# VectorE in place of GpSimd for two groups of additions in the first product of a gMLP decoder kernel

## The chip, the cores and the metric

The kernel runs on one core of one Trainium2 chip. The metric is the device time of one execution in microseconds (us), and the time of a kernel is the median of several runs. In the rows PE is TensorE's matmul, PEld its weight load, DVE is VectorE, ACT is ScalarE, POOL is GpSimd and SP is SyncE, whose queue (SPq) issues loads.

## What is computed

A decoder trunk of two layers on x (1 x 2048 tokens x 1024 features). The first layer is the one that matters here:

```python
def rms_norm(x, g):
    y = x * rsqrt(mean(x * x, axis=-1, keepdims=True) + EPS) * g
    return y

def gmlp_mixer(h, w_in, ln_g, ln_b, ws, bs, w_out):      # h = rms_norm(x, a_norm_g)
    z = h @ w_in                                         # (2048 x 1024) @ (1024 x 6144)
    u, v, g = jnp.split(z, 3, axis=-1)                   # 2048 columns each
    v = layer_norm(v, ln_g, ln_b)
    v = v.reshape(b, nc, CHUNK, A_GROUPS, A_GROUP_DIM)   # chunks of 128 tokens, 16 groups of 128
    sv = jnp.einsum('gts,bcsgd->bctgd', tril(ws), v) + bs.T[:, :, None]
    y = u * sv.reshape(b, s, A_WIDTH) * silu(g)
    return y @ w_out

h = x + gmlp_mixer(rms_norm(x, a_norm_g), ...)
```

After it come one product for keys and values, a sliding-window attention layer with its own in and out products, and a last norm. The change lies wholly in the first tenth of the run: the product that makes v for the first 1024 tokens, and what is prepared beside it.

## The kernel before

**Layout.** Activations lie with features on the 128 partitions and 512 tokens in the free direction. The 2048 tokens are four blocks of 512; two blocks make a superblock, and the gMLP layer runs superblock by superblock. Every operand of a large product is held as two float32r parts, hi and lo, and each product is three matmuls: hi by hi (L122), hi by lo (L123), lo by hi (L124). Both parts of a weight tile `wa` are made from the loaded float32 tile `w_raw`: ScalarE casts hi (L118) and VectorE subtracts to get lo (L119). There are four buffers for `wa`, so a split runs at most four weights ahead of the matmuls that use it, and L123 cannot run before its weight's L119.

**The first v product** (`vphase_first`, L591 to L608) takes x unnormalized, as hi and lo parts `xh`, `xl` times the gain (made at L750 and L751), and the token scale 1/rms is put on afterwards when ScalarE copies the product out of PSUM (L605). It runs four column groups by two token blocks by eight feature tiles k: 64 weights of 128 x 512, with twelve matmuls each. After each group of eight weights ScalarE copies four banks out and VectorE takes their statistics (`bn_stats`, L607). The product runs from 5.5 to 233 us of the span.

**Work put beside it.** The calls `after(n, ...)` place work at half-steps of the product (one half-step per weight). The scheduler that builds the program then orders each engine's instructions by its own estimate; the order below is the one that it chose. Beside the first v product stand:

- the norm of the first and second token block. `first_stat` (L766 to L774) squares each of eight tiles on ScalarE and adds the squares; `rnorm` (L266 on) splits the sum (hi by ScalarE, lo by GpSimd at L119), sums over partitions on TensorE (L270, L271), and makes the reciprocal root per token, `r4` (L255 to L260), and as a 128 x 512 tile, `r0` (L277 to L289). For the first block the squares are added on VectorE (`sumsq_step`, L248), for the second on GpSimd (L770).
- `x_steps(0, k)` for k = 0 to 3 (L424 to L463): four normalized quarters of x are made in a tile `xq`, and `combos` (L365 to L383) writes three of them to HBM and makes sums and differences of them on GpSimd (L373, L375, L379, L381), each written by a DMA that GpSimd's queue issues (L367). There are two `xq` buffers, so the third and fourth k must wait for the last combination (L381) and the DMAs of the first and second. Each quarter is made in two steps: an addition of its hi and lo part (L451), and a product with r0 (L452, VectorE).
- `sum_job(i)`, four jobs (L465 to L488): GpSimd makes sums and differences of weight tiles `qa`, eight additions each (L479), written by four DMAs (L472).
- `load_consts` (L385 to L406): tables for the token mixing (a matmul L398, VectorE L401, DMAs L403).

`in_turn` (L757 to L763) makes the GpSimd additions that pass through it follow one another in the order in which the code names them: L479, L451 and L770.

Of the kernel before, what the change touches and what calls it, by code (L numbers as in the profile page):

```python
# [12 lines left out]
F32 = mybir.dt.float32  # L13
F32R = mybir.dt.float32r
I32 = mybir.dt.int32
AF = mybir.ActivationFunctionType
ALU = mybir.AluOpType
# [45 lines left out]
def trunk(ctx: ExitStack, tc: tile.TileContext, xT, wv, wug, wao, wkv, wqg, wbo, wsT, bs, gains, lngb,  # L63
          bq, bkv, sinks, rot, masks, out):
    nc = tc.nc
    V, A, G, PE = nc.vector, nc.scalar, nc.gpsimd, nc.tensor
# [21 lines left out]
    def load(dst, src):  # L88
        nc.sync.dma_start(dst, src)

    def slot(dt=F32):
        return gen[0].tile([P, TB], dt, name="s", tag="s")
# [69 lines left out]
    for b in range(NB):  # L162
        for p in PIECES:
            kind, i, j = p[0], int(p[1]), int(p[2])
# [78 lines left out]
    def sumsq_step(acc, src, eng=G):  # L243
        sq = slot()
        A.activation(sq, src, AF.Square)
        if acc is None:
            return sq
        eng.tensor_tensor(acc, acc, sq, ALU.add)  # L248
        return acc
# [83 lines left out]
    with ExitStack() as actx:  # L333
# [31 lines left out]
        def combos(q11, q12, q21, q22, key, k):  # L365

            put = lambda n, t: G.dma_start(setD[key][n][:, k], t)  # L367
            put("11", q11)
            put("12", q21)
            put("s4", q22)  # L370
            yield
            t1, t2 = slot(), slot()
            G.tensor_tensor(t1, q12, q11, ALU.subtract)  # L373
            put("s1", t1)
            G.tensor_tensor(t2, q22, t1, ALU.subtract)  # L375
            put("s2", t2)
            yield
            t3, t4 = slot(), slot()
            G.tensor_tensor(t3, q22, q12, ALU.subtract)  # L379
            put("s3", t3)  # L380
            G.tensor_tensor(t4, q21, t2, ALU.subtract)  # L381
            put("22", t4)
            yield  # L383
# [40 lines left out]
        def x_steps(sb, k, tag):  # L424

            qs, its = [], []

            def begin():
                if sb == 0:
                    t = xcg.tile([P, 2048], F32, name="xq", tag=tag)  # L430
                    qs.extend(t[:, i * TB:(i + 1) * TB] for i in range(4))
                else:
                    qs.extend(slot() for _ in range(4))
                if sb:
                    for i, z in enumerate(qs):
                        load(z, xT[2 + i // 2, k + 4 * (i % 2)])
                    rs.extend(slot() for _ in range(2))
                    for h in range(2):
                        load(rs[h], rxD[2 + h])
                else:  # L440
                    rs.extend(r0[h] for h in range(2))

            rs = []

            def norm(i):
                h, n = i // 2, k + 4 * (i % 2)
                if sb:
                    V.scalar_tensor_tensor(qs[i], qs[i], a_g[:, n:n + 1], rs[h], ALU.mult, ALU.mult)
                else:
                    hi, lo = fx[h, n]  # L450
                    in_turn(lambda: G.tensor_tensor(qs[i], hi.bitcast(F32), lo.bitcast(F32), ALU.add))  # L451
                    V.tensor_tensor(qs[i], qs[i], rs[h], ALU.mult)  # L452

            def norms(h):
                norm(2 * h)
                norm(2 * h + 1)

            def step():
                if not its:
                    its.append(combos(qs[0], qs[2], qs[1], qs[3], ("X", sb), k))  # L460
                next(its[0])

            return [begin, lambda: None, lambda: None, lambda: norms(0), lambda: norms(1), step, step, step]  # L463
# [290 lines left out]
        box = [None, None]  # L754
        gl = [None]

        def in_turn(fn):  # L757

            if gl[0] is None:
                gl[0] = fn().ins  # L760
                return
            with tc.issue_after(gl[0]):
                gl[0] = fn().ins  # L763


        def first_stat(h, k, t, wait):  # L766
            if h and box[1]:
                sq = slot()
                A.activation(sq, t, AF.Square)
                in_turn(lambda: G.tensor_tensor(box[1], box[1], sq, ALU.add))  # L770
            else:
                box[h] = sumsq_step(box[h], t, V)
            if k == KD - 1:
                rnorm(box[h], lambda r: r0.update({h: r}), wait, 4, lambda z: r4.update({h: z}))  # L774

# [7 lines left out]
        for k in range(KD):  # L783
            after(ST0 + k // 2, lambda k=k: first_stat(0, k, xs[k], 1))
        ys = []
        for k in range(KD):
            after(1 + k // 2, lambda k=k: ys.append(first_x(1, k)))
            after(3 + k // 2, lambda k=k: first_split(1, k, ys[k]))
            after(6 + k // 2, lambda k=k: first_stat(1, k, ys[k], 2))
# [350 lines left out]
    for b in range(NB):  # L1140
# [39 lines left out]
        for p in PIECES:  # L1180
            kind, i, j = p[0], int(p[1]), int(p[2])
# [79 lines left out]
```

## Time and profile before

| | us |
|---|---|
| median of 3 runs | 2227.95 |
| the runs | 2225.21, 2227.95, 2232.17 |
| the profiled execution, its time | 2234.51 |
| the profiled execution, its span | 2232.8 |
| TensorE busy in the span | 2141.1 |
| VectorE busy | 1669.6 |
| GpSimd busy | 1092.5 |

The profiled execution is one run of its own, 6.6 us above the median of the others. TensorE is busy in all but 92 us of the span, so a stretch is read by how far TensorE falls short of the stretch's length there, and by what ended each of its idle times. In the first v product TensorE falls short in four places, near 45, 60 to 120, 132 and 155 to 170 us; after 170 us it runs without a gap until the product's end.

### The profile page before, as it was taken

The page shows a single profiled execution, that of the slowest core. Times are in us where ns is not written, and L with a number is a line of the kernel's source. Part 1 is how long each engine was busy: PE and PEld are TensorE (multiplying, and loading weights), DVE is VectorE, ACT ScalarE, POOL GpSimd, SP SyncE. Part 2 cuts the span into 40 slices and gives each one's busy share as a digit, 9 for nine tenths or more (in the row PEclk, how much of TensorE's full clock was granted, in tenths as well). Part 3 has the DMA queues.
Part 4 walks back from the last instruction along what each step waited for, and adds up shares of the span by engine and source line. Part 5 has one row for each costly group of instructions (what it writes and reads, how often), then busy time and mean ns, then how long its engine had stood idle before and what let it go on. Part 6 is the DMA issues. An engine that isn't in the chain of part 4 may idle for free.

```text
span 2232.8 us, 33563 instructions
## 1 busy us (share of the span) xinstructions
PE 2141.1 (96%) x11196; PEld 1813.6 (81%) x11196; DVE 1669.6 (75%) x2670; ACT 1088.6 (49%) x2431; POOL 1092.5 (49%) x1201
## 2 busy tenths in 40 slices
PE   7879999999899989999999899999999999999997
PEld 6658888888688767788888788898899889889986
DVE  7946787788986865756656977578867967986785
ACT  6224654445444534444444533246635734663573
POOL 4892355767444555644544545334514622551460
PEclk9989999999999999999999999999999999999999
DMA  8987555667786789634444786633363355337322
GB/s 283 342 298 238 180 185 188 208 196 244 256 303 226 273 312 314 222 113 135 149 133 130 263 309 214 214 123 114 123 245 115 115 187 180 114 124 243 116 95 95
DMA packets 208941, 441.96 MB, mean 198 GB/s; under 512 B 22656, under 2 KB 61824, under 8 KB 199552
## 3 DMA queue, kind: packets, MB, share of 16 engines
q1 hardware_dynamic: 163488, 255.76, 35.6%
q0 software_dynamic: 40672, 175.66, 21.5%
q10 hardware_dynamic: 4608, 8.39, 1.0%
q8 instruction: 89, 1.46, 0.3%
q14 instruction: 84, 0.69, 0.1%
HBM read 322.81 MB, written 116.92 MB: 197 GB/s over the span
## 4 chain that ended last, share of the span: by engine, by line
PE 72%; DVE 10%; DMA 7%; issue 5%; POOL 4%; ACT 2%; SPq 1%; POOLq 0%; DVEq 0%; ACTq 0%
PE ps L130 13%; PE ps L129 13%; PE ps L128 13%; PE ps L122 8%; PE ps L123 8%; PE ps L124 8%; PE ps L635 2%; PE ps L1024 2%; DVE wa L119 1%; PE ps L971 1%; PE ps L1002 1%; PE ps L972 1%; PE ps L943 1%; DMA s<-Y 1%; POOL qa L479 1%
## 5 line engine op out<-in xcount | busy, mean ns | idle before, releaser
L119 DVE TENSOR_TENSOR wa<-w_raw,wa 128x512 fp32r<-128x512 f32 x456 | 478.7, 1059 | 148.0 <-ACT wa L118 147.0
L130 PE MATMUL ps<-xh,wa 128*128 128x512 f32 x1344 | 529.4, 394 | 14.7 <-DVE wa L119 14.7
L128 PE MATMUL ps<-xh,wa 128*128 128x512 f32 x1344 | 531.2, 395 | 0.6 <-DVE s L656 0.3
L129 PE MATMUL ps<-xl,wa 128*128 128x512 f32 x1344 | 528.2, 393 | 0.0
L118 ACT CAST wa<-w_raw 128x512 fp32r<-128x512 f32 x456 | 280.6, 619 | 433.0 <-PE ps L130 314.9
L130 PEld LDWEIGHTS ps<-xh,wa 128*128 128x128 f32 x1344 | 253.3, 188 | 74.8 <-DVE wa L119 18.4
L128 PEld LDWEIGHTS ps<-xh,wa 128*128 128x128 f32 x1344 | 253.6, 189 | 56.6 <-DVE s L656 0.8
L129 PEld LDWEIGHTS ps<-xl,wa 128*128 128x128 f32 x1344 | 253.6, 189 | 55.7
L1010 POOL TENSOR_SCALAR_AFFINE_SELECT s<-s 128x512 fp32r<-128x512 f32 x256 | 185.0, 750 | 101.5 <-ACT s L1004 70.2
L223 POOL TENSOR_TENSOR w_raw<-w_raw 128x512 f32<-128x512 f32 x48 | 78.6, 1639 | 224.5 <-DMA w_raw<-in_wug 121.7
L122 PE MATMUL ps<-w,hn 128*128 128x256 f32 x640 | 184.5, 288 | 0.0
L123 PE MATMUL ps<-w,hn 128*128 128x256 f32 x640 | 182.6, 285 | 0.0
L124 PE MATMUL ps<-w,hn 128*128 128x256 f32 x640 | 182.5, 285 | 0.0
L119 DVE TENSOR_TENSOR xl<-s,xh 128x512 fp32r<-128x512 f32 x168 | 137.7, 856 | 13.7 <-ACT xh L118 13.6
L190 POOL DMA_DIRECT2D w<-wb x72 | 40.5, 563 | 208.8 <-PE ps L124 177.7
L631 ACT ACTIVATE vp<-vp,nb,rs 128x128 f32<-128x128 f32 x256 | 106.6, 485 | 46.0 <-DMA vp<-v 39.1
L123 PE MATMUL ps<-wa,xh 128*128 128x512 f32 x256 | 107.1, 418 | 21.2 <-DVE wa L119 20.9
L996 POOL TENSOR_TENSOR s<-s,rd 128x512 f32<-128x512 f32 x64 | 69.5, 1088 | 114.8 <-ACT s L1004 46.6
L123 PEld LDWEIGHTS ps<-w,hn 128*128 128x128 f32 x640 | 124.4, 194 | 0.5
L122 PEld LDWEIGHTS ps<-w,hn 128*128 128x128 f32 x640 | 124.2, 194 | 0.5
L124 PEld LDWEIGHTS ps<-w,hn 128*128 128x128 f32 x640 | 124.2, 194 | 0.0
L225 POOL TENSOR_TENSOR w_raw<-w_raw 128x512 f32<-128x512 f32 x48 | 65.1, 1362 | 104.7 <-DVE wa L119 102.4
(192 smaller groups left out, 5007.6 us busy)
## 6 DMA issues: line engine op xcount, KB each, us to landing
w<-wb POOLq DMA_DIRECT2D x72, 1024.0 KB, 5.5
w_raw<-in_wug SPq DMA_DIRECT2D x160, 256.0 KB, 3.2
w_raw<-in_wv SPq DMA_DIRECT2D x88, 256.0 KB, 5.4
s<-in_xT SPq DMA_DIRECT2D x80, 256.0 KB, 4.7
w_raw<-in_wao SPq DMA_DIRECT2D x80, 256.0 KB, 4.2
wb<-s POOLq DMA_DIRECT2D x72, 256.0 KB, 5.1
vp<-v SPq DMA_DIRECT2D x32, 512.0 KB, 4.4
Y_s<-s POOLq DMA_DIRECT2D x64, 256.0 KB, 3.9
```

The lines of the kernel that those rows point to most:

```text
L118: A.copy(hi, src)
L119: (lo_eng or V).tensor_tensor(lo, src, hi.bitcast(F32), ALU.subtract)
L122: PE.matmul(ps, ah, bh, start=first, stop=False)
L123: PE.matmul(ps, ah, bl, start=False, stop=False)
L124: PE.matmul(ps, al, bh, start=False, stop=last)
L128: PE.matmul(ps, ah, bh, start=first, stop=False, skip_group_check=True)
L129: PE.matmul(ps, ah, bl, start=False, stop=False, skip_group_check=True)
L130: PE.matmul(ps, al, bh, start=False, stop=True, skip_group_check=True)
L223: G.tensor_tensor(u["22"], u["21"], u["22"], ALU.add)
L631: A.activation(v[:, c, :], v[:, c, :], AF.Identity, bias=nb[:, c:c + 1], scale=rs[:, c:c + 1])
L996: G.tensor_tensor(p4, p4, rd[:, :, None].broadcast_to([P, 4, P]), ALU.mult)
L1010: G.affine_select(out=y.rearrange("p (h q) -> p h q", h=4), in_=x.rearrange("p (h q) -> p h q", h=4), pattern=[[0, 4], [sign, P]], base=ba ...
```

## The change

Two groups of additions move from GpSimd to VectorE. In `x_steps` the sixteen additions L451 leave GpSimd's fixed turn. In `first_stat` the second block's seven square additions (L770 with the squares of L769) go through `sumsq_step` as the first block's do, and so to VectorE's L248 (squares at L245).

```diff
             def norm(i):
                 h, n = i // 2, k + 4 * (i % 2)
...
                     hi, lo = fx[h, n]
-                    in_turn(lambda: G.tensor_tensor(qs[i], hi.bitcast(F32), lo.bitcast(F32), ALU.add))
+                    V.tensor_tensor(qs[i], hi.bitcast(F32), lo.bitcast(F32), ALU.add)
                     V.tensor_tensor(qs[i], qs[i], rs[h], ALU.mult)
...
         def first_stat(h, k, t, wait):
-            if h and box[1]:
-                sq = slot()
-                A.activation(sq, t, AF.Square)
-                in_turn(lambda: G.tensor_tensor(box[1], box[1], sq, ALU.add))
-            else:
-                box[h] = sumsq_step(box[h], t, V)
+            box[h] = sumsq_step(box[h], t, V)
             if k == KD - 1:
                 rnorm(box[h], lambda r: r0.update({h: r}), wait, 4, lambda z: r4.update({h: z}))
```

Every engine's order of instructions changes in the first v product alone; behind it the orders are the same, line for line. Three places follow, each of the kernel before and then of the changed one. Counted from the product's first, the split that stands behind all these additions in the first place is the 12th.

VectorE where the second block's norm is made, some 31 to 50 us into the span. L282 is the end of the first block's norm, L255 the first step of the second block's that reads TensorE's sum. Before:

```order
L282 TENSOR_TENSOR s<-ident,r4h 128x512
L282 TENSOR_TENSOR s<-ident,r4l 128x512
L119 TENSOR_TENSOR wa<-w_raw,wa 128x512 x2
L607 BN_STATS bst<-s 128x6 x4
L119 TENSOR_TENSOR wa<-w_raw,wa 128x512 x3
L255 TENSOR_TENSOR s<-ps,ident 128x512
```

Changed, from behind the same two L282, two L119, the first two L248 and one L451, which alternate:

```order
L248 TENSOR_TENSOR s<-s 128x512
L607 BN_STATS bst<-s 128x6
L248 TENSOR_TENSOR s<-s 128x512
L607 BN_STATS bst<-s 128x6
L248 TENSOR_TENSOR s<-s 128x512
L607 BN_STATS bst<-s 128x6 x2
L451 TENSOR_TENSOR xq<-xh,xl 128x512 x3
L248 TENSOR_TENSOR s<-s 128x512
L451 TENSOR_TENSOR xq<-xh,xl 128x512
L248 TENSOR_TENSOR s<-s 128x512
L119 TENSOR_TENSOR wa<-w_raw,wa 128x512 x4
L255 TENSOR_TENSOR s<-ps,ident 128x512
```

Between the second L282 and the third of the weight splits L119 there stood two L119 and four L607; now there stand, with those ahead of the rows, two L119, four L607, seven L248 and five L451.

GpSimd in the same stretch; `su` are the sums in HBM, and the second L119 is the lo part of the second block's sum of squares. Before:

```order
L119 TENSOR_TENSOR s<-s 128x512
L260 TENSOR_TENSOR r_474<-m_471,neghalf 128x4
L770 TENSOR_TENSOR s<-s 128x512 x7
L479 TENSOR_TENSOR qa<-qa 128x512 x3
L119 TENSOR_TENSOR s<-s 128x512
L472 DMA su_0_153<-qa 128x1024
```

Changed:

```order
L260 TENSOR_TENSOR r_474<-m_471,neghalf 128x4
L479 TENSOR_TENSOR qa<-qa 128x512 x2
L472 DMA su_0_153<-qa 128x1024
L479 TENSOR_TENSOR qa<-qa 128x512 x3
L472 DMA su_2_155<-qa 128x1024
L479 TENSOR_TENSOR qa<-qa 128x512 x2
L472 DMA su_1_154<-qa 128x1024
L479 TENSOR_TENSOR qa<-qa 128x512
L119 TENSOR_TENSOR s<-s 128x512
L472 DMA su_3_156<-qa 128x1024
```

The first job's eight additions and three of its DMA issues now stand ahead of that L119, in the place of seven L770 and three L479.

VectorE from the 28th weight split of the product to the 35th, some 105 to 140 us into the span; L401 belongs to `load_consts`. Before, with the third k of `x_steps`:

```order
L119 TENSOR_TENSOR wa<-w_raw,wa 128x512 x4
L401 SCALAR_TENSOR_TENSOR s<-ps,lngb_sb,s 128x128 x4
L119 TENSOR_TENSOR wa<-w_raw,wa 128x512 x2
L452 TENSOR_TENSOR xq<-xq,s 128x512
L119 TENSOR_TENSOR wa<-w_raw,wa 128x512
L452 TENSOR_TENSOR xq<-xq,s 128x512 x3
L119 TENSOR_TENSOR wa<-w_raw,wa 128x512
L401 SCALAR_TENSOR_TENSOR s<-ps,lngb_sb,s 128x128 x4
```

Changed, with the fourth k:

```order
L119 TENSOR_TENSOR wa<-w_raw,wa 128x512 x4
L401 SCALAR_TENSOR_TENSOR s<-ps,lngb_sb,s 128x128 x4
L451 TENSOR_TENSOR xq<-xh,xl 128x512 x2
L452 TENSOR_TENSOR xq<-xq,s 128x512
L119 TENSOR_TENSOR wa<-w_raw,wa 128x512
L452 TENSOR_TENSOR xq<-xq,s 128x512
L451 TENSOR_TENSOR xq<-xh,xl 128x512 x2
L452 TENSOR_TENSOR xq<-xq,s 128x512
L119 TENSOR_TENSOR wa<-w_raw,wa 128x512
L452 TENSOR_TENSOR xq<-xq,s 128x512
L119 TENSOR_TENSOR wa<-w_raw,wa 128x512 x2
L401 SCALAR_TENSOR_TENSOR s<-ps,lngb_sb,s 128x128 x4
```

In this stretch stood the third k, and the fourth stood about the 41st split; now the fourth k stands here, beginning ahead of the 32nd split, the third about the 24th and 25th, and behind the rows no L451 or L452 is left. The additions of the third and fourth k, which now stand in VectorE's order, wait there for the buffer: for L381 and the DMAs of the first and the second k.

## Rows read from the trace of the kernel before

**Rows 1.** The page's head: the span, and busy time of each engine (share of the span, instructions).

```profile
span 2232.8 us, 33563 instructions
...
PE 2141.1 (96%) x11196; PEld 1813.6 (81%) x11196; DVE 1669.6 (75%) x2670; ACT 1088.6 (49%) x2431; POOL 1092.5 (49%) x1201
```

**Rows 2.** Stretches of the span: its start and end, its length, busy time of PE, PEld, DVE, ACT and POOL with their instructions, TensorE's granted clock (1.00 is 2.4 GHz), the mean share of the DMA engines, and GB/s.

```profile
60.00:80.00 20.00, 18.31 (x75) 13.54 (x74) 20.00 (x15) 6.63 (x11) 16.59 (x19) 1.00 1.01 357
80.00:100.00 20.00, 16.66 (x68) 12.27 (x66) 18.00 (x10) 4.70 (x8) 19.05 (x21) 1.00 0.97 339
100.00:120.00 20.00, 17.02 (x57) 12.58 (x58) 17.11 (x23) 3.90 (x7) 14.89 (x17) 0.83 0.97 332
120.00:140.00 20.00, 14.94 (x52) 11.31 (x52) 9.85 (x13) 5.01 (x8) 19.58 (x20) 0.83 0.90 307
140.00:160.00 20.00, 15.44 (x66) 11.92 (x64) 4.39 (x7) 6.25 (x10) 19.66 (x20) 0.98 0.95 347
160.00:180.00 20.00, 16.57 (x60) 13.29 (x61) 17.18 (x16) 2.48 (x4) 15.06 (x16) 0.77 0.62 208
180.00:200.00 20.00, 20.00 (x89) 16.41 (x88) 10.85 (x17) 10.31 (x18) 0.00 (x0) 1.00 0.71 233
31.00:170.00 139.00, 112.88 (x422) 85.44 (x421) 101.05 (x94) 37.96 (x64) 125.85 (x123) 0.89 0.87 299
```

**Rows 3.** Waits from 40 to 180 us: the engine, tile and line that waited, what it waited for, us in total, times, the longest.

```profile
DVE xq L452 <- POOL xq L451: 28.7, 3, 14.4
...
PE ps L123 <- DVE wa L119: 20.9, 8, 7.8
...
PE ps L271 <- POOL s L119: 3.7, 1, 3.7
```

**Rows 4.** The timeline of TensorE in a few short stretches: start in the span, duration, engine, line, operation, tiles, shape, and in brackets the idle time before it and what ended that.

```profile
43.60 0.50 PE L270 MATMUL ps<-s,inv_r 128*128 128x512 f32 x1 [1.34 <-ACT s L118]
...
48.30 0.80 PE L271 MATMUL ps<-s,inv_r 128*128 128x512 f32 x1 [3.73 <-POOL s L119]
...
122.08 0.39 PE L123 MATMUL ps<-wa,xh 128*128 128x512 f32 x1
...
132.84 0.80 PE L123 MATMUL ps<-wa,xh 128*128 128x512 f32 x1 [5.06 <-DVE wa L119]
...
163.43 0.79 PE L123 MATMUL ps<-wa,xh 128*128 128x512 f32 x1 [7.83 <-DVE wa L119]
164.02 0.63 PE L124 MATMUL ps<-wa,xl 128*128 128x512 f32 x1
164.45 0.63 PE L122 MATMUL ps<-wa,xh 128*128 128x512 f32 x1
...
169.14 0.46 PE L124 MATMUL ps<-wa,xl 128*128 128x512 f32 x1
169.44 0.39 PE L122 MATMUL ps<-wa,xh 128*128 128x512 f32 x1
169.68 0.39 PE L123 MATMUL ps<-wa,xh 128*128 128x512 f32 x1
```

**Rows 5.** Groups of instructions from 0 to 180 us: line, engine, operation, tiles, shapes, count, then busy us and mean ns of one, then the idle time just before them and what ended it.

```profile
L119 DVE TENSOR_TENSOR wa<-w_raw,wa 128x512 fp32r<-128x512 f32 x48 | 68.2, 1448 | 5.8 <-ACT wa L118 5.8
L479 POOL TENSOR_TENSOR qa<-qa 128x512 f32<-128x512 f32 x32 | 43.6, 1388 | 1.8 <-DMA qa<-in_wv 1.7
...
L451 POOL TENSOR_TENSOR xq<-xh,xl 128x512 f32<-128x512 f32 x16 | 22.9, 1452 | 0.1
L607 DVE BATCH_NORM_STATS2 bst<-s 128x6 f32<-128x512 f32 x20 | 12.6, 676 | 0.0
L770 POOL TENSOR_TENSOR s<-s 128x512 f32<-128x512 f32 x7 | 11.2, 1595 | 1.3 <-ACT s L769 0.8
L472 POOL DMA_DIRECT2D su<-qa x16 | 9.3, 583 | 0.6 <-POOL qa L479 0.6
...
L248 DVE TENSOR_TENSOR s<-s 128x512 f32<-128x512 f32 x7 | 4.8, 683 | 0.0
```

**Rows 6.** The timeline of GpSimd and then of VectorE about the second block's norm, as in rows 4 (xN: so many of a kind in a row, with the time of all).

```profile
31.26 11.64 POOL L770 TENSOR_TENSOR s<-s 128x512 f32<-128x512 f32 x7 [0.84 <-ACT s L769]
...
46.99 1.25 POOL L119 TENSOR_TENSOR s<-s 128x512 fp32r<-128x512 f32 x1
```

```profile
31.81 1.79 DVE L282 TENSOR_TENSOR s<-ident,r4l 128x512 fp32r<-128x512 f32 x1
33.52 3.47 DVE L119 TENSOR_TENSOR wa<-w_raw,wa 128x512 fp32r<-128x512 f32 x2
36.91 2.46 DVE L607 BATCH_NORM_STATS2 bst<-s 128x6 f32<-128x512 f32 x4
39.30 2.47 DVE L119 TENSOR_TENSOR wa<-w_raw,wa 128x512 fp32r<-128x512 f32 x2
```

**Rows 7.** The timeline of VectorE, then of GpSimd, at the third and fourth k and in the dense stretch ahead of them, as in rows 4.

```profile
71.71 12.72 DVE L119 TENSOR_TENSOR wa<-w_raw,wa 128x512 fp32r<-128x512 f32 x4
...
130.15 0.96 DVE L452 TENSOR_TENSOR xq<-xq,s 128x512 f32<-128x512 f32 x1 [12.31 <-POOL xq L451]
...
160.54 1.17 DVE L452 TENSOR_TENSOR xq<-xq,s 128x512 f32<-128x512 f32 x1 [14.41 <-POOL xq L451]
```

```profile
119.73 1.33 POOL L381 TENSOR_TENSOR s<-xq,s 128x512 f32<-128x512 f32 x1
...
159.25 1.25 POOL L451 TENSOR_TENSOR xq<-xh,xl 128x512 f32<-128x512 f32 x1
```

## The prediction, made before the changed kernel ran

> **What bounds the kernel now.** I read the head of the page first: TensorE is busy 96% of the span [rows 1], so only its gaps are to be had. By stretches, the first v product has its gaps before 170 us; from 180 us TensorE is busy 20.00 of 20.00 us at the full clock [rows 2]. The changed kernel has the same order of instructions from there on, so what is won before 170 us is kept, and nothing can be won later.
>
> The waits name the last thing that TensorE waited for in 40 to 180 us: mostly a weight's lo part, L119 on VectorE, 20.9 us; once the lo part of the second block's sum of squares on GpSimd, 3.7 us; and VectorE itself stood 28.7 us in L452, waiting for GpSimd's L451 [rows 3]. A split that stands behind such an L452 is late by that wait. The four places, with TensorE's loss in each:
>
> The low clock first. After the 7.83 us gap the matmuls start 0.43 us apart (164.02, 164.45) until 169.14, then 0.24 apart (169.44, 169.68) [rows 4]: the granted clock has gone to the lower of its two levels, 1.2 GHz, and comes back to 2.4 after 5.7 us, some 13 matmuls, which cost 13 x 0.19 = 2.5 us. The first matmul behind the gaps at 48 and 132 us takes 0.80 as here, and the granted clock of 100 to 120 us is 0.83 [rows 2, 4], so I count 2.5 at each place.
>
> Place 1, the second block's norm: idle 1.34 + 3.73 = 5.1 [rows 4], with the clock 7.6. Place 2, 60 to 120 us: short of 20 by 1.69, 3.34 and 2.98 [rows 2], 8.0, with the clock 10.5. Place 3, 132.84: 5.06 [rows 4], 7.6. Place 4, 140 to 180: short by 4.56 and 3.43 [rows 2], 8.0, with the clock 10.5. All four are 36.2 us, the most that the change can bring.
>
> **The change part by part.** What an addition costs on VectorE: L248, the same operation and shape with GpSimd quiet, takes 0.68 us and starts 0.6 after the one before; on GpSimd L451 took 1.45 and L770 1.60 [rows 5]. But beside GpSimd's run of L770 VectorE's operations of two SBUF inputs took 1.7 each (1.79; 3.47 for two), while four L607, with one SBUF input, kept 0.6 [rows 6]; in the dense stretch four L119 took 12.72, or 3.2 each [rows 7]. So 0.6, 1.7 and 3.2 are the three prices of a moved addition.
>
> Place 1. Behind the L282 at 31.81 VectorE now has, itself included, 15 operations of two inputs and four L607 before the 12th split, the last of them the last L248. GpSimd, which did seven L770 from 31.26, does eight L479 instead, with three DMA issues of 0.58 among them: 8 x 1.66 (11.64 / 7, beside a busy VectorE) + 1.7 = 15.0, to 46.3 [rows 5, 6]. In the 14.5 us to there VectorE gets through four L607 (2.4), seven operations at 1.7 and about two in the gaps of the DMA issues; the six left cost 0.6 each, and the last L248 ends at 49.9. The hi cast (0.7), the lo part on GpSimd (1.25 [rows 6]) and a handover bring L271 to 51.9, where it started at 48.30: 3.6 us lost. Bounds: with no interference GpSimd's eight additions end at 31.26 + 8 x 1.39 + 1.7 = 44.1, L271 runs at 45.4, a gain of 2.9; at 3.2 each VectorE has done four or five by 46.3, and L271 runs at 54.4, a loss of 6.1. I take 3.6, by the rows of this very place. What queues behind: the 12th to 15th splits, for which TensorE waits in any case behind L271, and L452 of the first k.
>
> Place 2. Eight L451 leave GpSimd (8 x 1.45 = 11.6 us) and come to VectorE, in a stretch where both are busy nearly throughout (55.1 and 50.5 of 60 us [rows 2]). If each takes the place of a GpSimd operation and costs 0.68, both together gain 8 x 0.77 = 6.2; at 1.7 they lose 2.0. I take the middle, 2.1 gained, 8.4 of loss left; the bounds are a loss of 8 x 3.2 - 11.6 = 14 and the whole 10.5. The third k's additions stand here now, and wait for the first k's L381, ahead of the 24th split.
>
> Place 3. Here stood the third k, held because L451 had its turn behind GpSimd's L479. Now the fourth k stands here: ahead of the 32nd split two L451 wait for the L381 of the second k, which ended at 119.73 + 1.33 = 121.06 [rows 7]. TensorE wanted that split at 122.08 [rows 4]. GpSimd has 7 x 1.60 + 8 x 1.45 less to do before that L381 and four L479 and three DMA issues more (4 x 1.39 + 1.7), so it ends up to 15.5 us earlier, at 105.5, if GpSimd waits for nothing new: no loss at all. If it stays at 121.06, two L451, one L452 and the split at 0.6 to 1.7 end at 123.5 to 127.9: up to 5.8 idle and 2.5 of clock. I take the middle of nothing and the old 7.6: 3.8 gained.
>
> Place 4. No L452 or L451 is left beyond the 36th split, so the wait of 14.41 us at 160.54 [rows 7] has nothing to stand in: 9.5 of 10.5 gained, one us kept for GpSimd's late L479, which still stretch L119; bounds 7.5 and 10.5.
>
> The start. Two L451 stand among the very first splits, where TensorE waits for loads and splits: 0 to 2 x 0.68, taken as 0.5 lost. The DMA issues of the x quarters (L367) and of the sums (L472) move earlier with their data, into stretches whose DMA share is already 0.97 to 1.01 [rows 2]; the weights' loads share these engines, but in these stretches the splits wait for GpSimd, not for a load, so this is counted at nothing; if that cover goes, a late load costs part of place 2's loss again, within its bounds. ScalarE does the same squares as before.
>
> Sum: -3.6 + 2.1 + 3.8 + 9.5 - 0.5 = 11.3 us gained. The profiled execution, 2234.5, is 6.6 above the median of 2227.95; against itself it would come to 2223, and against the median to 2217.
>
> **The rivals.** *VectorE becomes the bound.* In 31 to 170 us it is not busy for 139 - 101.05 = 38.0 us [rows 2], of which 28.7 were waits for L451 [rows 3] and so are free to use. After 31 us it takes on seven L248 and fourteen L451, 21 operations: 1.8 us each is the point from which it has no room, and every split behind comes late. The price beside L770 was 1.7, in the dense stretch 3.2; at the middle, 2.45, it is 21 x 0.65 = 13 us over, and the kernel takes 2241. For it speak the 20.00 of 20.00 us in 60 to 80; against it that GpSimd has 16 x 1.45 + 7 x 1.60 = 34 us less in which to hold VectorE up.
>
> *The wait is only renamed.* The additions of the third and fourth k stand in VectorE's own queue for GpSimd's L381, which now has four more L479 ahead of it and waits for VectorE's L452. Then place 2 and place 3 keep their losses, place 1 loses its upper 6.1, and only place 4 is won: -6.1 + 9.5 - 0.5 = 2.9, 2225. Perfetto Trace Analysis, section Optimizing Scalar/DVE Operations, in the Trainium skill, speaks for this side: it says that work moved between GpSimd and VectorE might not help, since they share a read port.
>
> *The freed time is all passed on.* GpSimd's 34 us less against VectorE's 21 x 0.68 = 14 us more leave 20 us in which neither holds the other; the splits of places 2 and 3 are then in time, and only places 1 and the start lose: 10.5 + 7.6 + 9.5 - 4.1 = 23.5, 2204.
>
> That the additions don't move is excluded: the new order shows them on VectorE.
>
> **How the numbers follow.** About 0.3% (6.7 us) is what a measurement of this kernel can tell from no change. The forecast, 2217, has 0.38; its own bounds are about 2211 to 2225, and some 0.26 of its chance lies below 2221. The passed-on time, 2204, has 0.22; the renamed wait, 2225, 0.21; VectorE as the bound, 2241, 0.19. Faster is 0.26 + 0.22 + a little of the renamed wait, 0.49; slower is VectorE as the bound, 0.19, and 0.01 of the rest, 0.20; the same is 0.31. Leaving out the better half of the fastest case and the worse half of the slowest gives 2203 to 2238.
>
> **What would show it.** Place 1: L271 for the second block near 52 us, with VectorE's L248 ahead of it stretched while GpSimd runs L479; right if later than 48.3, wrong if at 45. Place 2: the idle time of TensorE in 60 to 120 us near 6 to 8. Place 3: what ends the wait of the L451 at the 32nd split, and whether L381 of the second k ends near 106 or 121. Place 4: no gap beyond 140 us. VectorE as the bound would show as splits late with VectorE never idle in 45 to 130 us; the renamed wait as idle time of VectorE put down to L381. The prediction is wrong if the moved additions cost above 1.8 us each, or if a place behind 170 us shows a new gap.

## The result and the profile after

The changed kernel takes 2237.49 us (median of 6 runs, 2233.68 to 2241.00) against 2228.41 of the kernel before (6 runs, 2225.21 to 2232.17): a ratio of 1.0039, 95% interval 1.0026 to 1.0051. It is slower by 9.1 us where 11 us less were forecast.

All of it is in the first v product. Its last matmul starts at 232.38 us before and at 241.22 now, 8.8 us later:

```profile
232.38 0.40 PE L124 MATMUL ps<-wa,xl 128*128 128x512 f32 x1
```

```profile
241.22 0.40 PE L124 MATMUL ps<-wa,xl 128*128 128x512 f32 x1
```

What lies behind it took 2000 us of the profiled execution before and 1995 in that of the changed kernel; over the traces of all sixteen kernels of this document it lies between 1990 and 2003. So the experiments are compared by ratios of medians, and within the first v product by the trace.

The stretches of the changed kernel, columns as in [rows 2]:

```profile
40.00:60.00 20.00, 13.00 (x37) 9.27 (x38) 17.99 (x25) 4.01 (x7) 7.26 (x6) 0.67 0.48 157
...
80.00:100.00 20.00, 15.36 (x62) 11.23 (x60) 9.28 (x15) 3.31 (x6) 13.61 (x18) 1.00 0.99 361
100.00:120.00 20.00, 11.48 (x33) 8.83 (x34) 20.00 (x19) 3.26 (x5) 16.87 (x17) 0.66 0.83 282
...
140.00:160.00 20.00, 12.18 (x44) 9.60 (x45) 19.79 (x22) 4.51 (x7) 16.92 (x18) 0.74 0.74 261
160.00:180.00 20.00, 20.00 (x88) 16.31 (x87) 12.04 (x11) 6.88 (x11) 12.38 (x14) 1.00 0.91 316
31.00:170.00 139.00, 103.54 (x386) 79.26 (x385) 106.95 (x113) 34.58 (x58) 98.52 (x102) 0.85 0.83 293
```

160 to 180 us is now full; three holes are new, in 35 to 60, about 100 and about 140 us. In 31 to 170 us VectorE is still not busy for 32 us (21.9 of them in waits, below), and GpSimd is busy for 98.5 us instead of 125.9: neither engine has become the bound. The waits from 40 to 180 us say what did:

```profile
PE ps L123 <- DVE wa L119: 26.9, 7, 11.1
...
DVE xq L451 <- POOL s L381: 21.9, 2, 11.2
...
PE ps L289 <- DVE s L282: 6.9, 1, 6.9
```

The 28.7 us in which L452 waited for L451 [rows 3] are gone. In their place L451 waits 21.9 us for L381, in two waits; and TensorE waits 6.9 us for L282, which was no wait before.

**The first hole: one operation held for 8.3 us.** VectorE at the end of the first block's norm, then GpSimd:

```profile
33.94 0.68 DVE L282 TENSOR_TENSOR s<-ident,r4h 128x512 fp32r<-128x512 f32 x1
34.55 8.30 DVE L282 TENSOR_TENSOR s<-ident,r4l 128x512 fp32r<-128x512 f32 x1
42.76 1.75 DVE L119 TENSOR_TENSOR wa<-w_raw,wa 128x512 fp32r<-128x512 f32 x1
44.44 0.68 DVE L248 TENSOR_TENSOR s<-s 128x512 f32<-128x512 f32 x1
```

```profile
34.31 0.77 POOL L472 DMA_DIRECT2D su<-qa  x1 [0.31 <-POOL qa L479]
35.10 3.72 POOL L479 TENSOR_TENSOR qa<-qa 128x512 f32<-128x512 f32 x3
38.77 0.57 POOL L472 DMA_DIRECT2D su<-qa  x1
39.36 2.49 POOL L479 TENSOR_TENSOR qa<-qa 128x512 f32<-128x512 f32 x2
41.79 0.57 POOL L472 DMA_DIRECT2D su<-qa  x1
42.38 1.58 POOL L479 TENSOR_TENSOR qa<-qa 128x512 f32<-128x512 f32 x1
```

The second L282 begins inside a DMA issue of GpSimd and ends 8.30 us later, at 42.85, 0.49 us behind the end of the third issue of the rows; between, GpSimd does five L479 at 1.24 to 1.25 us, no slower than the 1.30 of the one at 127.09 below, when VectorE stood idle. The sixth, in whose time L282 ends, takes 1.58. The same L282 took 1.79 in the kernel before [rows 6], where GpSimd ran seven L770 at 1.66 each and let it and the next two L119 in within 1.8 us each. Behind it stand a split that TensorE needs, the seven L248 and the five L451, and behind those the 12th split. What TensorE waited for there:

```profile
42.90 0.80 PE L289 MATMUL ps<-s,ones_r 128*128 128x512 f32 x1 [6.94 <-DVE s L282]
...
55.37 0.51 PE L123 MATMUL ps<-wa,xh 128*128 128x512 f32 x1 [1.99 <-DVE wa L119]
...
58.29 0.80 PE L271 MATMUL ps<-s,inv_r 128*128 128x512 f32 x1 [1.66 <-POOL s L119]
```

**The other two: L381 comes late, and two operations behind it are held.** VectorE at the third and fourth k; then GpSimd:

```profile
98.41 1.73 DVE L451 TENSOR_TENSOR xq<-xh,xl 128x512 f32<-128x512 f32 x2 [10.72 <-POOL s L381]
...
101.10 5.50 DVE L119 TENSOR_TENSOR wa<-w_raw,wa 128x512 fp32r<-128x512 f32 x1
...
137.68 2.82 DVE L451 TENSOR_TENSOR xq<-xh,xl 128x512 f32<-128x512 f32 x2 [11.19 <-POOL s L381]
140.43 5.49 DVE L452 TENSOR_TENSOR xq<-xq,s 128x512 f32<-128x512 f32 x1
145.85 1.75 DVE L119 TENSOR_TENSOR wa<-w_raw,wa 128x512 fp32r<-128x512 f32 x1
```

```profile
55.44 2.80 POOL L119 TENSOR_TENSOR s<-s 128x512 fp32r<-128x512 f32 x1 [11.48 <-ACT s L118]
...
90.43 0.63 POOL L393 TENSOR_SCALAR_AFFINE_SELECT s<-s 128x512 f32<-128x512 f32 x1 [6.36 <-DMA s<-in_wsT]
...
97.11 1.27 POOL L381 TENSOR_TENSOR s<-xq,s 128x512 f32<-128x512 f32 x1
...
101.81 3.81 POOL L479 TENSOR_TENSOR qa<-qa 128x512 f32<-128x512 f32 x3
...
127.09 1.30 POOL L479 TENSOR_TENSOR qa<-qa 128x512 f32<-128x512 f32 x1 [4.60 <-DMA qa<-in_wv]
...
132.05 0.63 POOL L393 TENSOR_SCALAR_AFFINE_SELECT s<-s 128x512 f32<-128x512 f32 x1 [3.16 <-DMA s<-in_wsT]
...
136.36 1.29 POOL L381 TENSOR_TENSOR s<-xq,s 128x512 f32<-128x512 f32 x1
...
141.10 3.79 POOL L479 TENSOR_TENSOR qa<-qa 128x512 f32<-128x512 f32 x3
```

GpSimd had less to do and came no earlier, for in its own order it stood waiting. From 28 us to the end of the second k's L381, at 137.65 where the old one ended at 121.06 [rows 7], it was idle for 41.2 us in the changed kernel's trace and for 16.2 in that of the kernel before. Of the 25 us more, 11.5 are the wait of its L119 for ScalarE's hi part of the second block's sum of squares, which comes late with the first hole. Another 10.1 are waits for loads (14.1 against 4.0): 6.4 us ahead of the first k's L381, 4.6 and 3.2 ahead of the second's. The load that L393 waited for was issued late, because on SP's queue it stands behind loads of `qa` that must wait until the sums of the job before are written. SP's wait from 72 to 84 us, and the issues behind it:

```profile
SPq L89 <- DMA su<-qa: 10.7, 2, 6.6
```

```profile
83.47 0.38 SPq L89 DMA_DIRECT2D qa<-in_wv  x1
83.90 0.50 SPq L89 DMA_DIRECT2D s<-in_wsT  x1
```

The splits behind the two L451 came 9.5 and 11.1 us late for TensorE, at 106.66 and 147.65. So TensorE wanted them at 97.2 and 136.6, and the two L381 ended only 1.2 and 1.1 us after that. The rest is the time of two L451, an L452 and the split: 8.2 and 9.9 us, where four such operations undisturbed take some 2.5. In each hole one of them was held for 5.5 us, through three L479: the split at 101.10 and the L452 at 140.43. Without these holds the same late L381 would have cost some 4 us of idle time at each place, an estimate from the 0.6 us at which such operations follow each other when GpSimd is quiet.

Prices, from 0 to 180 us. The moved additions were cheap, L451 at 1.02 us and L248 at 0.68, and L119 fell from 1448 ns [rows 5] to 1036. The means hide the single long ones, the L282 of 8.30 and the L119 of 5.50:

```profile
L119 DVE TENSOR_TENSOR wa<-w_raw,wa 128x512 fp32r<-128x512 f32 x45 | 45.5, 1036 | 7.8 <-ACT wa L118 5.7 <-DMA w_raw<-in_wv 2.1
...
L451 DVE TENSOR_TENSOR xq<-xh,xl 128x512 f32<-128x512 f32 x16 | 15.8, 1018 | 21.9 <-POOL s L381 21.9
...
L248 DVE TENSOR_TENSOR s<-s 128x512 f32<-128x512 f32 x14 | 9.6, 684 | 0.0
```

**TensorE's loss by weight.** For the comparisons below: the time between the starts of the matmuls of the first v product beyond 0.2335 us each (their distance at full clock), summed over stretches of the 64 weights, in us. The sixteen other matmuls that stand among them count at the same 0.2335, the low clock after a hole is in it, and the last row has weights 44 to 64 too. Columns are the kernel before, the changed one, and six of the runs that follow. A trace is of one execution, which can lie some us from its kernel's median (that of job_late4, 2212.25 us, is the fastest of its ten), so losses and times agree only to a few us.

| weights | before | changed | sq_only | x_only | xq4 | job0_late | job123_late | job_late4 |
|---|---|---|---|---|---|---|---|---|
| 1 to 8 | 3.7 | 3.9 | 3.4 | 2.7 | 2.2 | 3.6 | 3.5 | 3.2 |
| 9 to 13 | 7.8 | 17.2 | 10.4 | 9.8 | 15.3 | 9.2 | 16.3 | 9.4 |
| 14 to 23 | 3.4 | 2.2 | 7.0 | 1.0 | 9.0 | 0.1 | 1.5 | 4.4 |
| 24 | 0.4 | 12.1 | 0.4 | 13.2 | 1.8 | 9.2 | 5.2 | 2.7 |
| 25 to 31 | 10.1 | 4.0 | 14.9 | 3.9 | 9.3 | 0.5 | 0.3 | 8.9 |
| 32 | 0.4 | 13.7 | 4.4 | 8.8 | 0.4 | 11.2 | 13.9 | 0.7 |
| 33 and 34 | 7.3 | 0.3 | 4.0 | 0.2 | -0.1 | 6.6 | 4.2 | 0.1 |
| 35 to 43 | 11.6 | -0.2 | 6.4 | -0.2 | -0.2 | 0.3 | -0.2 | -0.2 |
| all | 44.0 | 52.6 | 50.3 | 38.8 | 37.1 | 40.0 | 44.2 | 28.8 |

### The profile page after: what moved, and what is told of

Its sections match the earlier page's. It is cut to its first block, busy times and chain, and to the rows that moved or that the text cites. A ratio compares the mean times of both kernels' runs of the same rounds, so it can differ in the third digit from the quotient of the medians.

```text
span 2236.3 us, 33562 instructions
## 1 busy us (share of the span) xinstructions
PE 2135.4 (95%) x11196; PEld 1811.6 (81%) x11196; DVE 1675.6 (75%) x2693; ACT 1088.7 (49%) x2431; POOL 1057.7 (47%) x1178
## 4 chain that ended last, share of the span: by engine, by line
PE 71%; DVE 11%; DMA 6%; issue 5%; POOL 3%; ACT 2%; SPq 1%; DVEq 0%; POOLq 0%; ACTq 0%
PE ps L130 13%; PE ps L129 13%; PE ps L128 13%; PE ps L122 8%; PE ps L124 8%; PE ps L123 8%; PE ps L635 2%; PE ps L1019 2%; DVE wa L119 1%; PE ps L997 1%; PE ps L966 1%; PE ps L967 1%; DMA s<-Y_s 1%; DMA s<-in_xT 1%; PE ps L938 1%
## 5 line engine op out<-in xcount | busy, mean ns | idle before, releaser
L119 DVE TENSOR_TENSOR wa<-w_raw,wa 128x512 fp32r<-128x512 f32 x456 | 449.6, 996 | 154.7 <-ACT wa L118 149.3
L130 PE MATMUL ps<-xh,wa 128*128 128x512 f32 x1344 | 530.1, 394 | 16.4 <-DVE wa L119 16.4
L223 POOL TENSOR_TENSOR w_raw<-w_raw 128x512 f32<-128x512 f32 x48 | 76.0, 1585 | 231.1 <-DMA w_raw<-in_wug 145.3
L119 DVE TENSOR_TENSOR xl<-s,xh 128x512 fp32r<-128x512 f32 x168 | 138.9, 865 | 17.2 <-ACT xh L118 17.0
L118 ACT CAST xh<-s 128x512 fp32r<-128x512 f32 x168 | 97.1, 617 | 36.7 <-DMA s<-Y 11.4
```

What stands on the lines that cost most here:

```text
L118: A.copy(hi, src)
L119: (lo_eng or V).tensor_tensor(lo, src, hi.bitcast(F32), ALU.subtract)
L130: PE.matmul(ps, al, bh, start=False, stop=True, skip_group_check=True)
L223: G.tensor_tensor(u["22"], u["21"], u["22"], ALU.add)
```

## The experiments

Each is timed against the kernel before on the same chip, whose median there was 2229 to 2230 us; ratios are to that, with the 95% interval.

**x_only.** One half of the change: the diff's first piece, with L770 left on GpSimd.

```diff
-                    in_turn(lambda: G.tensor_tensor(qs[i], hi.bitcast(F32), lo.bitcast(F32), ALU.add))
+                    V.tensor_tensor(qs[i], hi.bitcast(F32), lo.bitcast(F32), ALU.add)
```

> Only the sixteen additions L451 are on VectorE; the second block's squares are added on GpSimd as before. Theory A: the changed kernel lost its time to three waits: the r4l product L282 held up by the first job's additions L479 on GpSimd (9.4 us more lost at the second block's norm than before), and the additions of the third and of the fourth k, which stand in VectorE's queue ahead of weight splits and wait for GpSimd's L381 (12 and 13 us lost at the 24th and 32nd weight). Here the first is gone, since GpSimd runs L770 there again, the two others stay: 2226 to 2230 us. Rival B: each moved addition costs VectorE and the splits behind it a little, so the loss goes with their number, 16 of 23: 2234 to 2236.

2228.39 us, 0.9988 (0.9969 to 1.0008): as theory A has it. The loss at weights 9 to 13 is down to 9.8; the two waits for L381 stand, 21.4 us together. So L451 on VectorE alone neither gains nor loses: what goes at weights 25 to 43 comes back at the 24th and 32nd.

**sq_only.** The other half: the diff's second piece alone.

> Only the second block's seven square additions are on VectorE; L451 stays on GpSimd in its fixed turn. Theory A: the L282 is held up as in the changed kernel, some 8 us of waiting, and the waits of L452 for L451 are those of the kernel before: 2236 to 2240 us. Rival B: 7 of 23 moved additions: 2230 to 2232, without a place that stands out.

2241.57 us, 1.0055 (1.0037 to 1.0072): by its time on theory A's side, a little beyond its range. By time the squares' move alone makes the whole loss. But not at the place that theory A named: weights 9 to 13 lose 10.4, only 2.6 more than before, and 8.4 more are lost at weights 14 to 31. And what is held is another operation; L282 took 1.78, and the split behind it 5.55, again from a DMA issue of GpSimd on, through the same three L479:

```profile
32.64 1.78 DVE L282 TENSOR_TENSOR s<-ident,r4l 128x512 fp32r<-128x512 f32 x1
34.34 5.55 DVE L119 TENSOR_TENSOR wa<-w_raw,wa 128x512 fp32r<-128x512 f32 x1
```

The mean of L119 is 1802 ns there, so more is held than at one place.

**xq4.** The changed kernel with four `xq` buffers (in a part of the on-chip memory that is free until later).

```diff
-            for i, f in enumerate(x_steps(0, k, ("12h", "12l")[k % 2])):
+            for i, f in enumerate(x_steps(0, k, ("12h", "12l", "s2h", "s2l")[k])):
```

> The changed kernel with four xq buffers in place of two, so that no addition of the third and fourth k waits for L381. Theory A: the losses of 12 and 13 us at the 24th and 32nd weight go, the one at the second block's norm stays: 2210 to 2216 us. Rival B (VectorE is the bound, L381 is only what happens to end last): the additions come earlier still and the splits are as late: 2233 to 2240.

2227.38 us, 0.9987 (0.9971 to 1.0002). The waits for L381 are gone, and 0.5% against the changed kernel's 1.0039, some 11.6 us, come back: the waits, with what stood behind them, were a cause. Only half of what theory A forecast, for 12 us are lost elsewhere: the additions stand earlier, and other holds (an L119 of 7.75 us in GpSimd's next run of L479, among them) cost TensorE 6.8 us more at weights 14 to 23 and 5.3 at 25 to 31. VectorE is not the bound (rival B), but neither does it have all that room at all times.

**job_late4.** The changed kernel with the four sum jobs four half-steps later.

```diff
-            after(14 + 9 * i, lambda i=i: sum_job(i))
+            after(18 + 9 * i, lambda i=i: sum_job(i))
```

> The changed kernel with the four sum jobs placed four half-steps later, so that the first job's loads land behind the end of the first block's norm. Theory A: L282 takes under 2 us and the loss at the second block's norm falls from 17 us to 8 to 12, the waits for L381 stay within 3 us of theirs: 2228 to 2234 us. Rival B: GpSimd's work is only shifted, 2236 to 2239.

2218.74 us, 0.9949 (0.9931 to 0.9967): beyond theory A's range, and faster than both kernels. L282 takes 0.68, and the loss at weights 9 to 13 is 9.4, as forecast; but the waits for L381 fell too, which was not:

```profile
DVE xq L451 <- POOL s L381: 5.5, 2, 4.7
```

**before_jl4 and x_only_jl4.** The same later jobs in the kernel before and in x_only.

> The kernel before, with nothing moved to VectorE, with the four sum jobs four half-steps later as in the run job_late4. Theory A: the jobs' place is worth little by itself, since L451 still has its turn behind L479: 2223 to 2230 us, and job_late4's gain needs the moved additions. Rival D: the jobs' place alone gives the gain: 2214 to 2221.

> L451 alone on VectorE (squares added on GpSimd), with the sum jobs four half-steps later. If the squares on VectorE cost something by themselves, this beats job_late4 by 5 us or more: 2207 to 2214 us. If their cost in the changed kernel was only that GpSimd's first job started 12 us earlier, it equals job_late4: 2215 to 2222.

before_jl4: 2236.27 us, 1.0036 (1.0018 to 1.0054), slower than either theory has it. x_only_jl4: 2227.02 us, 0.9993 (0.9978 to 1.0009), above both ranges. So with the jobs later the moves are worth 1.0036 to 0.9949, 0.87% or 19 us, and the squares' half of it 0.44%; with the jobs in their old place the same squares cost 0.51% (1.0039 against x_only's 0.9988). What the squares' move does depends on what GpSimd does in the time that it is given.

**consts_36.** The changed kernel with `load_consts` at half-steps 36 to 48 in place of 14 to 26, so that L393 and its load are out of the way.

```diff
-            after(14 + 4 * q, lambda q=q: load_consts(q))
+            after(36 + 4 * q, lambda q=q: load_consts(q))
```

> The changed kernel with the tables of load_consts made 22 half-steps later, so that no L393 and no wait of it for its load stands on GpSimd ahead of the combinations of the first and second k. Theory A: the third and fourth k's additions wait for L381, and L381 is late because L393 ahead of it waits for a load that SP's queue issues late (6.4 us ahead of the first k's, 3.2 ahead of the second's): the two waits of L451 fall from 21.9 us together to 8 to 14 and the time to 2222 to 2230. Rival C: L381 is late because GpSimd simply has that much work ahead of it: waits above 18 us, 2233 to 2240.

2234.29 us, 1.0009 (0.9989 to 1.0030): the waits of L451 are 12.1 us together, in theory A's range, and the time is in rival C's. The third k no longer waits, since the first k's L381 ends at 87.7 where it ended at 98.4, so that one was not late through GpSimd's work. The fourth waits 12.1 us, since GpSimd now stood 8.6 us ahead of an L479; the profile puts that down to a store of v, but the job's last loads of `qa` were issued only at 114.35, 3.2 us before that L479 began, so I take it that they ended it, which is not shown. And the time follows the waits only in part: the losses at weights 24 and 32 fall from 25.8 together to 4.4, and 16 us more are lost at weights 14 to 23 and 25 to 31. So a load had a part in the first L381's lateness, and with it out of the way the next wait comes forward.

**puts_turn.** The changed kernel with the four DMA issues of a sum job held, by `in_turn`, behind its eight additions.

```diff
             tt(a22, a21, a22, ALU.add)
-            put(0, a22)
             tt(a21, a11, a21, ALU.subtract)
-            put(2, a21)
...
             tt(a12, a12, a11, ALU.subtract)
-            put(3, a12)
+            in_turn(lambda: put(0, a22))
+            in_turn(lambda: put(2, a21))
...
```

> The changed kernel with the four DMA issues of a sum job held back behind its eight additions, so that GpSimd runs eight additions without a break at the second block's norm. Theory P: VectorE gets in between two GpSimd additions as long as it asks while one runs, and misses its turn only when it asks while GpSimd issues a DMA: L282 below 2 us, the loss at the second block's norm falls by 8 to 12: 2226 to 2232. Rival Q: VectorE waits for a break in GpSimd's run, and the DMA issues are the breaks: one operation of VectorE takes 9 us or more there, 2236 to 2244.

2226.69 us, 0.9977 (0.9962 to 0.9991). Where the hold was, theory P is right: beside eight L479 without a break every operation of VectorE takes its turn.

```profile
33.51 1.78 DVE L282 TENSOR_TENSOR s<-ident,r4l 128x512 fp32r<-128x512 f32 x1
35.22 1.76 DVE L119 TENSOR_TENSOR wa<-w_raw,wa 128x512 fp32r<-128x512 f32 x1
```

```profile
29.89 13.36 POOL L479 TENSOR_TENSOR qa<-qa 128x512 f32<-128x512 f32 x8
```

The loss at weights 9 to 13 fell only from 17.2 to 14.0, though, not by 8 to 12: the eight turns and the L248 ahead of the 12th split keep that split late. The time is in theory P's range for another reason: the losses at the 24th and 32nd weight fell from 25.8 together to 3.2, and the waits of L451 for L381 from 21.9 to 9.7, which the theory did not forecast. Later in the same run an L119 that began inside an addition was held 6.4 us, so the theory's rule is not the whole of it.

**before_puts_turn, jl4_puts_turn, xq4_puts_turn, jl4_xq4_puts.** The same order of the DMA issues in the kernel before, in job_late4, in xq4, and in both together.

> The kernel before, nothing moved to VectorE, with the DMA issues of the sum jobs behind their eight additions. Theory P: the 3.2 us of a split in the dense stretch of the kernel before come from splits that asked during a DMA issue; the mean of L119 on VectorE falls from 1448 ns to under 1250, and the time to 2216 to 2225. Rival Q: it is the number of GpSimd's additions that counts: mean above 1350 ns, 2226 to 2234.

> The changed kernel with the sum jobs four half-steps later and their DMA issues behind their additions. Theory P: VectorE's waits of over 3 us go here too, some 3 to 8 us below job_late4, which was 0.9949 of the kernel before: 2207 to 2216. If the DMA issues matter only at the end of the first block's norm, where job_late4 has none, there is no gain: 2216 to 2222.

> The changed kernel with both removed at once: four xq buffers, so that no addition waits for L381, and the DMA issues of the sum jobs behind their additions. Theory A+P: the two are separate causes; against the kernel before, the ratio of the first alone was 0.9987 and of the second 0.9977, where the changed kernel had 1.0039; if the gains add, this has 0.9925, 2210 to 2217 us. Rival E: what one gives the other takes, since the splits then wait for VectorE's other work: 0.9965 or above, 2222 to 2230.

> All three together: sum jobs four half-steps later, their DMA issues behind their additions, four xq buffers. If the waits of the third and fourth k for L381 are the last of the new losses, this is the fastest: 2202 to 2212 us. Rival E as for the first of these runs: 2214 or above.

2242.53 us, 1.0054 (1.0036 to 1.0071); 2239.50, 1.0048 (1.0032 to 1.0065); 2226.86, 0.9990 (0.9979 to 1.0001); 2241.34, 1.0055 (1.0040 to 1.0070). What theory P forecast fails in all four, and rival E stands: the gains don't add. In the kernel before the mean of L119 went up, to 1756 ns. A run of additions without a break can let VectorE take turns, and it can hold VectorE through eight operations. In jl4_puts_turn VectorE had been taking turns with two L479, began its next split inside a DMA issue, and was let in again after eight operations of GpSimd; VectorE, then GpSimd:

```profile
150.70 11.20 DVE L119 TENSOR_TENSOR wa<-w_raw,wa 128x512 fp32r<-128x512 f32 x1
```

```profile
150.17 0.72 POOL L403 DMA_DIRECT2D wsc<-s  x1
150.86 5.06 POOL L479 TENSOR_TENSOR qa<-qa 128x512 f32<-128x512 f32 x4
155.84 1.30 POOL L373 TENSOR_TENSOR s<-xq 128x512 f32<-128x512 f32 x1
157.06 1.29 POOL L479 TENSOR_TENSOR qa<-qa 128x512 f32<-128x512 f32 x1
...
158.85 1.28 POOL L375 TENSOR_TENSOR s<-xq,s 128x512 f32<-128x512 f32 x1
160.07 1.27 POOL L379 TENSOR_TENSOR s<-xq 128x512 f32<-128x512 f32 x1
```

**job0_late and job123_late.** To part the two things that job_late4 removed: the changed kernel with the first job alone four half-steps later, and with the other three alone.

```diff
-            after(14 + 9 * i, lambda i=i: sum_job(i))
+            after(14 + 9 * i + 4 * (i == 0), lambda i=i: sum_job(i))
```

For job123_late the condition is `i > 0`.

> The changed kernel with the first sum job alone four half-steps later. Theory F: what the squares' move costs is that GpSimd begins the first job's additions 12 us earlier, beside the end of the first block's norm; holding back that job alone gives most of the gain of job_late4 (0.9949 of the kernel before): 0.994 to 0.998, 2216 to 2225 us. Rival G: the gain came from the later jobs, whose loads then stand behind those of load_consts in SP's queue, so that L393 and with it L381 come earlier: 1.001 or above, 2231 to 2239.

> The changed kernel with the second to fourth sum job four half-steps later and the first in its place. Theory F: VectorE's operation at the end of the first block's norm is held up as in the changed kernel, and the time stays at 1.001 of the kernel before or above: 2231 to 2240 us. Rival G: the waits of L451 for L381 fall below 10 us together and the time to 0.994 to 0.998: 2216 to 2225.

2230.23 us, 1.0002 (0.9988 to 1.0016), and 2230.64 us, 0.9998 (0.9983 to 1.0013): neither theory alone, each thing is about half. In job0_late the hold is gone and the waits for L381 stand:

```profile
31.70 0.68 DVE L282 TENSOR_TENSOR s<-ident,r4l 128x512 fp32r<-128x512 f32 x1
```

```profile
DVE xq L451 <- POOL s L381: 21.6, 2, 12.7
```

8.0 us come back at weights 9 to 13, and 0.37%, 8.2 us, in the time. That the two agree so well is in part chance, for the whole loss of this trace fell by 12.6. In job123_late the hold stands, and the loss at the 24th weight falls from 12.1 to 5.2, while that at the 32nd stays at 13.9 and the waits for L381 are still 17.3 us together, where rival G had them below 10:

```profile
L282 DVE TENSOR_TENSOR s<-ident,r4l 128x512 fp32r<-128x512 f32 x2 | 11.7, 5840 | 0.0
```

It gives 0.41%, 9.1 us. Together that is 0.78%, and job_late4, which does both, has 0.90%.

## Why the prediction was wrong

Its sum was right about what goes and wrong about what comes. By its own places, in us of TensorE's loss (a gain is positive):

| place | weights | loss before, forecast / measured | change forecast | change measured |
|---|---|---|---|---|
| 1, second block's norm | 9 to 13 | 7.6 / 7.8 | -3.6 | -9.4 |
| 2, 60 to 120 us | 14 to 31 | 10.5 / 13.9 | +2.1 | -4.4 |
| 3, 132 us | 32 to 34 | 7.6 / 7.7 | +3.8 | -6.3 |
| 4, 140 to 180 us | 35 to 43 | 10.5 / 11.6 | +9.5 | +11.8 |

With half a us at the start that is 8.8 lost in place of 11.3 gained.

**Place 4** held by its weights: no L452 is left there, and no gap beyond 160 us. Its sign, no gap beyond 140 us, did not, since place 3's hole now ends at 147.65.

**Place 3** is the step that failed most. Its 3.8 us gained rest on the second k's L381 ending between 105.5 and 121.06, for which it counted GpSimd's work only: seven L770 and eight L451 less, four L479 and three DMA issues more, "if GpSimd waits for nothing new". L381 ended at 137.65, outside the bounds, because GpSimd stood idle 25 us more ahead of it: in its own order it waits for ScalarE's part of the second block's sum, and for loads that SP issues in order behind others that wait for GpSimd's sums. The bound at 121.06 was no bound: that L381 comes no later than before was assumed. Against TensorE, which had itself lost time by then, L381 was late by little: it ended 1.0 us before TensorE wanted the split in the kernel before (122.08) and 1.1 us after it now. What made 11.1 us of idle time of it is the second term, the price behind the wait: two L451, one L452 and the split were given 2.4 to 6.8 us and took 9.9, with the L452 held for 5.5.

**Place 2** failed the same way: the third k's wait for the first k's L381 was named in a sentence and had no price in the sum; it was 10.7 us of VectorE's time, and with the L119 that was held for 5.5 us behind it 12.1 of TensorE's. TensorE was short by 13.2 us in 60 to 120, all of it in 80 to 120, where the sign was 6 to 8. The rival of the renamed wait named the waits and had 0.21, but it let places 2 and 3 keep their losses, where they lost 10.7 us more, and its 2225 was missed too. xq4 and job123_late show that the waits, with what stood behind them, were a cause; consts_36 shows that a load made the first L381 late, and that taking it away is not enough.

**Place 1** had the sign and not the size. L271 was forecast at 51.9 and came at 58.29, 6.4 us later. The hold of L282, 8.30 us where 1.7 was allowed, makes 6.6 alone; three other errors of the working cancel by luck. L282 began 2.7 us later than in the kernel before, all from its end to the last L248 took 11.9 us where the working has 16.4, since GpSimd's additions ended at 43.96, and the way from there to L271 took 3.6 in place of 2.0. The prices allowed were 0.6, 1.7 and 3.2; 3.2 was a mean over four splits, where the longest single split of that stretch in the kernel before, at 85.99, took 6.61. In job0_late, without the hold, 8 us of the loss at this place are gone.

**The rivals.** VectorE as the bound is excluded: the moved additions cost 0.68 and 1.02, below the 1.8 at which it would have decided, and of the 32 us in which VectorE was not busy only 21.9 were waits for L381; with those waits gone, in xq4, the kernel got faster and VectorE still had 19.8 us free in 31 to 170. The passed-on time exists: L119's mean fell by 0.4 us, but in the changed kernel the holds and the two waits ate it. job_late4, with little of either, comes to 2218.7 where 2217 was forecast. That is chance more than a late success: it is another kernel, and by places it loses 16.0 at weights 14 to 31, where 8.4 were forecast, and 0.8 at 32 to 34, where 3.8 were. Neither of the two signs that the prediction named for itself, a price above 1.8 us or a gap behind 170 us, was seen: a mean price could not show what single holds do.

Perfetto Trace Analysis, section Optimizing Scalar/DVE Operations, in the Trainium skill, which says that moving work between these two engines might not help, is borne out with the jobs in their old place (1.0039) and not with the jobs later (0.9949 against 1.0036 without the move).

**What stays open.** Why VectorE takes turns with one run of GpSimd's additions and is held by the next. How a VectorE operation begins tells something, counted over the first 180 us of all sixteen traces, for operations of two 128 x 512 inputs in the on-chip memory. All 711 that began while GpSimd was in none of its instructions took under 0.8 us. Of 373 that began inside a DMA issue of GpSimd 124 took over 2.2 us, and of 357 that began inside one of its 128 x 512 additions 39 did; in the changed kernel these are 9 of 23 and none of 18, in the kernel before 10 of 22 and 3 of 24. So a start inside a DMA issue is held more often, but most such starts are not held, and puts_turn and the runs after it show that moving the DMA issues does not do away with the holds. The size of such a hold could not have been computed, only allowed for.

## What to carry to other kernels

When an operation leaves an engine, look at what that engine now does in the freed time, and beside whom: here the seven additions that went had let VectorE take turns, and of the eight that took their place five held it up. When a wait is moved into another engine's queue, follow the awaited instruction back through every in-order queue ahead of it, the loads included, before giving it an early bound, and price what stands behind the wait, since it starts beside whatever the other engine does next; the work counted on its own engine says little. And a mean over stretched instructions is no price for one of them: read the single rows, and take the longest as the bound where one stands on the critical chain.

## What the runs showed of the hardware that was not expected

An operation of VectorE with two inputs in the on-chip memory was held for 8.30 us through five, and for 11.20 us through eight of GpSimd's operations, which took 1.24 to 1.30 us each and so were not slowed. In other runs of the same additions the two engines took turns, one operation each, in 1.66 to 1.79 us a pair. SBUF — State Buffer, section Summary: rules for kernel authors, in the Trainium skill, says that of two such operations the second to issue is blocked until the first has finished. Here L282 was the first of the two by the profile's starts, 0.55 us before the first of the five additions, and ended only behind the fifth. So the measurement differs from the rule, and decides.
